# A decoder layer's opening: the third weight's low part moved ahead of the second chunk's average, the fourth weight's first accumulator moved to another PSUM bank, and the first adaLN stage moved to the head of the queue

## The chip, the cores and the metric

One Trainium2 chip, one of its cores. The metric is the device time of one execution in microseconds; a kernel is timed several times and its median is given. The trace comes from one further execution under the hardware profiler.

## The reference

One layer of a decoder trunk for 1024 prompt rows and 8 x 8 sample rows of width 1024, in float32. The opening that the change touches computes, of the reference:

```python
mod = jax.nn.silu(c) @ ada_w[l] + ada_b[l]
shift1, scale1, gate1, shift2, scale2, gate2 = jnp.split(mod, 6, axis=-1)
h = rms_norm(x, norm1_g[l]) * (1.0 + scale1[:, None]) + shift1[:, None]
z = h @ w_in[l]
...
c_y, conf_new = causal_dwconv(c_a * jax.nn.sigmoid(c_b), conf_buf, conf_dw[l])
```

Behind it come retention, sliding-window attention, the convolutions, the output projection and the feed-forward part; the change leaves them as they are.

## The kernel before

**Layout.** The 1088 rows of x stand as columns in `M`, one slice of 128 features each for k = 0 to 7, in three chunks of 384, 384 and 320 columns (`CH`, line 24). A float32 product is made of three products of a reduced format: each operand is split into a high part (a cast on ScalarE) and a low part (a subtraction on VectorE), and TensorE adds high x high, high x low and low x high. `weight_split` (line 245) does this for a block of `w_in`: the cast runs at once, the subtraction at once or, where a list `later` is given, when it is popped from the list. A block of `w_in` is one transfer of 128 x 1024 floats, 512 KB.

**The norm.** `norm1_squares` (438) squares x on ScalarE and adds pairs on VectorE; `norm1` (457) sums them over the features with four products by a matrix of ones, and `rstd` (291) makes the reciprocal root: two functions on ScalarE, three operations on VectorE. `make_h` (471) then makes, for some k, the normed, scaled and shifted x: one multiplication on VectorE (`tmp`), one activation on ScalarE (`hi`), one operation on VectorE (`lo`).

**adaLN in stages.** The first two of the six parts of `mod` are made in four stages of two k each (378). A stage's 2 MB come as four transfers of 512 KB (`stage_load`, 382); stages 0 and 2 use the same room, and so do 1 and 3. `stage_sum` (406) is 32 small products, `stage_copy` (413) a copy on ScalarE, `stage_finish` (420) four products that add pairs, and two operations on VectorE that write shift and scale.

**The order.** From line 987 to 1094 `pinned` is set: ScalarE and VectorE run what stands there in the order of the program, as TensorE does everywhere. Behind line 1094 the order of those two engines is left to the builder, but for the steps of the long convolution (lines 602 to 614), which keep theirs. Transfers are issued by SP, in a queue of its own: x of the first chunk, the first weight, stage 0, the second weight, stage 1, x of the second chunk (397 to 402), the third weight, then what lines 1025 to 1037 ask for. `keep_warm(n)` (990) issues n float32 products that nobody reads, each of which runs as two passes.

**Accumulators.** PSUM has eight banks of 512 columns. `mm_psum` (230) goes round four of them, `misc_psum` (235) round two of the other four until line 1084; the last two are held for the second chunk. The first three weights' accumulators for the first chunk (996) are open from the start. The fourth weight's (1087) is next in the round and so takes the bank of the first weight's, which `evac_c` empties with a sigmoid (588). That sigmoid stands behind the third chunk's norm and a load of its function table (1077 to 1080).

**Around the change** (lines 1020 to 1094): squares and norm of chunk 0, stage 0, h of k 0 and 1, products of the first two weights with it; stage 1, h of k 2 and 3 while the second chunk is squared; norm of the second chunk; h of the second chunk, and so on in turn. The first weight is prepared at line 1022, the second at 1029, with its low part popped between the two weights' products; the third's low part is popped behind the second chunk's norm:

```python
        prepare(2, rest)
        norm1(1, (1, 2, 3))
        rest.pop()()
        make_h(1, (0, 1))
        part(0, (2,), range(4))
```

Of the kernel before, what the change touches and what calls it, by code (L numbers as in the profile page):

```python
# [23 lines left out]
CH = [(0, 384), (384, 384), (768, 320)]  # L24
# [116 lines left out]
def decoder_step(ctx: ExitStack, tc: tile.TileContext, A, O, where):  # L141
# [41 lines left out]
    def nm(s):  # L183
        serial[0] += 1
        return f"{s}_{serial[0]}"
# [10 lines left out]
    def table(name):  # L196
        load = ACT.preload_act_table_set(name)
        for n in group["users"] + ([group["load"].ins.name] if group["load"] else []):
            tc.add_manual_dep(load.ins, n, after, reason="table")
        group["load"], group["users"] = load, []  # L200
# [25 lines left out]
    def bank(kind, n=4):  # L226
        turn[kind] += 1
        return pp.tile([P, 512], F32, tag=f"{kind}{turn[kind] % n}", name=nm(kind))

    def mm_psum(w):  # L230
        return bank("mm")[:, :w]
# [3 lines left out]
    def misc_psum():  # L235
        return bank("pm", misc_banks[0])


    def weight(src, lo_engine, raw=None):
        if raw is None:  # L240
            raw = wp.tile([P, 1024], F32, tag="w", name=nm("w"), bufs=2)
        nc.sync.dma_start(raw, src)
        return raw, lo_engine

    def weight_split(raw, lo_engine, both=None, later=None):
        if both is None:
            hi = wp.tile([P, 1024], F32R, tag="wh", name=nm("wh"), bufs=2)
            lo = wp.tile([P, 1024], F32R, tag="wl", name=nm("wl"), bufs=2)
        else:
            hi, lo = both  # L250
        ACT.copy(hi, raw)
        rest = lambda: lo_engine.tensor_tensor(out=lo, in0=raw, in1=hi, op=ALU.subtract)
        if later is None:
            rest()
        else:
            later.append(rest)
        return hi, lo
# [19 lines left out]
    def act_of(tiles, c):  # L277
        return lambda k: (tiles[c][k // 4][0][:, k % 4, :], tiles[c][k // 4][1][:, k % 4, :])
# [12 lines left out]
    def rstd(ps, w, r, t, e=0):  # L291

        ev = EPS if e == 0 else EPS / 4
        act(r, ps, AF.Ln, bias=eps[:, e : e + 1])
        act(r, r, AF.Exp, scale=-0.5)
        DVE.scalar_tensor_tensor(t, ps, ev, r, ALU.add, ALU.mult)
        DVE.scalar_tensor_tensor(t, t, -0.5, r, ALU.mult, ALU.mult)
        DVE.scalar_tensor_tensor(r, t, 1.5, r, ALU.add, ALU.mult)
# [30 lines left out]
    with ExitStack() as gctx:  # L329
# [5 lines left out]
        def tmp(w=384, dtype=F32):  # L335
            return gp.tile([P, 384], dtype, tag="tmp", name=nm("tmp"), bufs=8)[:, :w]
# [15 lines left out]
        def fetch(i):  # L352
            if i < len(IN_BLOCKS) and i not in loaded:
                raw = None
                if i in (2, 3):
                    tag, n = (("u1", 2 + SEQ + NB * 10), ("t5", NT))[i - 2]
                    raw = gp.tile([P, n], F32, tag=tag, name=nm("w"))[:, 0:1024]
                loaded[i] = weight(A["w_in"][i], DVE, raw)

        def wide(dtype=F32):  # L360
            return gp.tile([P, 1028], dtype, tag="sw", name=nm("sw"), bufs=3)

        def flip(dtype=F32):
            return gp.tile([P, 1024], dtype, tag="pT", name=nm("pT"))

        def prepare(i, later=None):
            if i < len(IN_BLOCKS) and i not in ready:
                fetch(i)
                both = None
                if i == 4:  # L370
                    both = [gp.tile([P, n], F32R, tag=f"t{t}", name=nm("ak"))[:, 0:1024] for t, n in ((4, NT), (5, 1024))]
                elif i in (2, 3, 20, 21):
                    both = (wide(F32R)[:, 0:1024], wide(F32R)[:, 0:1024] if i in (2, 20) else flip(F32R))
                ready[i] = weight_split(*loaded[i], both, later)
                fetch(i + 1)
# [6 lines left out]
        def stage_load(s):  # L382
            k0, k1 = STAGES[s]
            for x, tag in enumerate(ROOM[s]):
                if tag[0] == "t":
                    t = gp.tile([P, NT if tag < "t3" else 1024], F32, tag=tag, name=nm("ada0"))[:, 0:1024]
                else:
                    t = hp.tile([P, 1024], F32, tag=tag, name=nm("ada0"))
                if s < 2:
                    src = A["ada_0"][:, 0:8192].rearrange("p (a k) -> p a k", k=512)[:, 4 * x : 4 * x + 4, k0 * P : k1 * P]  # L390
                    nc.sync.dma_start(t.rearrange("p (a k) -> p a k", a=4), src)  # L391
                else:
                    nc.sync.dma_start(t, A["ada_0"][:, 1024 * (4 * s + x) : 1024 * (4 * s + x + 1)])
                for y in range(4):
                    stage_tiles[s, 4 * x + y] = t[:, 256 * y : 256 * y + 256]

        fetch(0)
        stage_load(0)
        fetch(1)
        stage_load(1)  # L400
        for k in (0, 4):
# [36 lines left out]
        def norm1_squares(c, ks=range(8)):  # L438

            c0, w = CH[c]  # L440
            qs = squares.setdefault(c, [])
            if c < 2 and c not in square_rooms:
                room = [gp.tile([P, 30 + SEQ + NB * 38], F32, tag=f"glu{j}", name=nm("sq")) for j in range(2)]
                square_rooms[c] = [room[j][:, x * w : (x + 1) * w] for j in range(2) for x in range(3)]
            for k in ks:
                q = square_rooms[c][k] if c < 2 and k < 6 else tmp(w)
                ACT.activation(q, M[:, k, c0 : c0 + w], AF.Square)
                if k % 2:
                    DVE.tensor_tensor(out=qs[-1], in0=qs[-1], in1=q, op=ALU.add)
                    if c == 2 and k > 1:  # L450
                        DVE.tensor_tensor(out=qs[0], in0=qs[0], in1=qs.pop(), op=ALU.add)
                else:
                    qs.append(q)
# [3 lines left out]
        def norm1(c, xs=range(4), between=lambda x: None):  # L457
            c0, w = CH[c]
            if c not in sums1:
                sums1[c] = misc_psum()[:, :w]  # L460
            ps, n = sums1[c], len(squares[c]) if c == 2 else 4
            for x in xs[:n]:
                PE.matmul(ps, ones, squares[c][x], start=x == 0, stop=x == n - 1)
                between(x)
            if xs[-1] < 3:
                return
            rstd(ps, w, r1_all[:, c0 : c0 + w], tmp(w))
# [522 lines left out]
        def keep_warm(n, warm=warm):  # L990

            for _ in range(n):
                PE.matmul(warm, ones, ones, start=True, stop=True)

        misc_banks[0] = 2
        acc = {(0, n): mm_psum(CH[0][1]) for n in range(3)}
        free = ["pm2", "pm3"]
        rest = []
        hh, hl, lh = (0, 0), (0, 1), (1, 0)
        count = {}  # L1000

        def terms(c, n, ks, ts):

            ps = acc[c, n]
            for k in ks:
                for i, j in ts:
                    x = count[c, n] = count.get((c, n), 0) + 1
                    PE.matmul(ps, ready[n][i][:, k * P : k * P + P], act_of(h, c)(k)[j], start=x == 1, stop=x == 24)

        def part(c, ns, ks):  # L1010
            for k in ks:
                for n in ns:
                    terms(c, n, (k,), (hh, hl, lh))

        def stage(s):
            ps = misc_psum()
            stage_sum(s, ps)
            return stage_copy(s, ps)

        keep_warm(24)  # L1020
        norm1_squares(0)
        prepare(0)
        norm1(0, between=lambda x: keep_warm(4) if x == 1 else None)
        flat = stage(0)
        stage_load(2)
        keep_warm(5)
        stage_finish(0, flat)
        make_h(0, (0, 1))
        prepare(1, rest)
        keep_warm(8)  # L1030
        part(0, (0,), (0, 1))
        rest.pop()()
        part(0, (1,), (0, 1))
        flat = stage(1)
        stage_load(3)
        fetch(3)
# [9 lines left out]
        keep_warm(5)  # L1046
        part(0, (0, 1), (2, 3))
        prepare(2, rest)
        norm1(1, (1, 2, 3))
        rest.pop()()  # L1050
        make_h(1, (0, 1))
        part(0, (2,), range(4))
        acc[1, 0] = mm_psum(CH[1][1])
# [21 lines left out]
        names = IN_BLOCKS[:4]  # L1075
        part(1, range(3), (6, 7))
        norm1(2)
        table("sigmoid_and_others")
        for n in range(3):
            evac_c(names[n], 0, *CH[0], acc[0, n])  # L1080
# [3 lines left out]
        misc_banks[0] = 4  # L1084
        make_h(2, range(4))
        for c in range(2):
            acc[c, 3] = mm_psum(CH[c][1])
            part(c, (3,), range(8))
            evac_c(names[3], c, *CH[c], acc[c, 3])
            make_h(2, (4 + 2 * c, 5 + 2 * c))  # L1090
# [116 lines left out]
    with ExitStack() as fctx:  # L1207
# [12 lines left out]
        def wide_room(tag):  # L1220
            return up.tile([P, NT], F32, tag=tag, name=nm(tag), bufs=1)
# [187 lines left out]
        acc = wide_room("acc")  # L1409
# [57 lines left out]
        for g in range(NG - 1):  # L1467
# [84 lines left out]
            last = g + 1 == NG - 1  # L1552
# [146 lines left out]
```

## Time and profile before

| | |
|---|---|
| median of 3 runs | 1231.94 us (1231.42 to 1233.59) |
| the profiled execution | 1229.62 us |
| its span, first to last instruction | 1227.6 us |
| mean granted clock of TensorE | 0.997 |
| busy: TensorE, VectorE, ScalarE | 1206.9, 809.7, 464.9 us |
| bytes moved | 113.72 MB, 93 GB/s over the span |

Busy times are sums over the whole span; the opening, the first 90 us or so, has other limits than the rest. The granted clock is 1.00 at 2.4 GHz and 0.50 at 1.2 GHz. All times below are microseconds from the first instruction. Matrix products overlap in the pipeline, so their starts tell more than their lengths.

### The profile page before, as it was taken

The page shows a single profiled execution, that of the slowest core. Times are in us where ns is not written, and L with a number is a line of the kernel's source. Part 1 is how long each engine was busy: PE and PEld are TensorE (multiplying, and loading weights), DVE is VectorE, ACT ScalarE, POOL GpSimd, SP SyncE. Part 2 cuts the span into 40 slices and gives each one's busy share as a digit, 9 for nine tenths or more (in the row PEclk, how much of TensorE's full clock was granted, in tenths as well). Part 3 has the DMA queues.
Part 4 walks back from the last instruction along what each step waited for, and adds up shares of the span by engine and source line. Part 5 has one row for each costly group of instructions (what it writes and reads, how often), then busy time and mean ns, then how long its engine had stood idle before and what let it go on. Part 6 is the DMA issues. An engine that isn't in the chain of part 4 may idle for free.

```text
span 1227.6 us, 17259 instructions
## 1 busy us (share of the span) xinstructions
PE 1206.9 (98%) x7058; PEld 1096.8 (89%) x7058; DVE 809.7 (66%) x1288; ACT 464.9 (38%) x941; POOL 8.5 (1%) x28
## 2 busy tenths in 40 slices
PE   8899999999999999999999999999999999999998
PEld 6787789988899999998999999999999999999887
DVE  4669798884797447736476566566666566566575
ACT  4452333342367324633433333333233333333330
POOL 0000000000000000000000000000000000000000
PEclk9999999999999999999999999999999999999999
DMA  9728811121120723111221211212211221121332
GB/s 344 263 93 316 228 52 52 39 52 35 36 71 18 261 74 116 58 35 52 69 69 52 73 66 62 76 52 70 69 68 53 69 86 52 53 86 52 120 125 90
DMA packets 60165, 113.72 MB, mean 93 GB/s; under 512 B 13495, under 2 KB 29623, under 8 KB 60087
## 3 DMA queue, kind: packets, MB, share of 16 engines
q1 hardware_dynamic: 59943, 112.56, 28.0%
q8 instruction: 55, 0.90, 0.3%
q14 instruction: 23, 0.19, 0.1%
q10 hardware_dynamic: 144, 0.07, 0.0%
HBM read 101.90 MB, written 10.72 MB: 92 GB/s over the span
## 4 chain that ended last, share of the span: by engine, by line
PE 88%; DVE 7%; ACT 2%; SPq 1%; DMA 1%; issue 1%; DVEq 0%
PE ps L171 48%; PE mm L171 30%; PE pm L171 6%; DVE x L158 3%; PE sm L171 3%; PE pm L175 1%; PE ada L171 1%; DMA M<-in_xT 1%; SPq L391 1%; DVE al L158 1%; DVE ql L158 1%; ACT ah L158 1%; ACT q L158 0%; DVE qh L305 0%; DVE lo L312 0%
## 5 line engine op out<-in xcount | busy, mean ns | idle before, releaser
L171 PE MATMUL ps<-hi,wl 128*128 128x384 f32 (+1 forms) x672 | 219.5, 327 | 0.0
L171 PE MATMUL ps<-hi,wh 128*128 128x384 f32 (+1 forms) x672 | 219.3, 326 | 0.0
L171 PE MATMUL ps<-lo,wh 128*128 128x384 f32 (+1 forms) x672 | 219.1, 326 | 0.0
L171 PE MATMUL mm<-hi,wh 128*128 128x384 f32 (+1 forms) x544 | 181.4, 333 | 0.0
L171 PE MATMUL mm<-hi,wl 128*128 128x384 f32 (+1 forms) x544 | 177.6, 326 | 0.6 <-DVE wl L158 0.6
L171 PE MATMUL mm<-lo,wh 128*128 128x384 f32 (+1 forms) x544 | 177.5, 326 | 0.2 <-DVE lo L158 0.2
L158 ACT ACTIVATE q<-ps 128x384 f32<-128x384 f32 (+1 forms) x112 | 42.5, 380 | 351.7 <-PE ps L171 351.7
L158 DVE TENSOR_TENSOR x<-x,ps 128x512 f32<-128x512 f32 x264 | 165.1, 679 | 0.4 <-PE ps L171 0.4
L171 PE MATMUL ps<-qh,al 128*128 128x512 f32 x408 | 159.6, 391 | 0.0
L171 PE MATMUL ps<-ql,ah 128*128 128x512 f32 x408 | 159.5, 391 | 0.0
L171 PE MATMUL ps<-qh,ah 128*128 128x512 f32 x408 | 158.9, 389 | 0.0
L171 PEld LDWEIGHTS ps<-hi,wh 128*128 128x128 f32 x672 | 126.2, 188 | 2.2
L171 PEld LDWEIGHTS ps<-lo,wh 128*128 128x128 f32 x672 | 126.1, 188 | 2.2
L171 PEld LDWEIGHTS ps<-hi,wl 128*128 128x128 f32 x672 | 126.1, 188 | 0.0
L171 PEld LDWEIGHTS mm<-hi,wh 128*128 128x128 f32 x544 | 102.1, 188 | 8.0 <-issue 6.8
L171 PEld LDWEIGHTS mm<-hi,wl 128*128 128x128 f32 x544 | 102.1, 188 | 0.9 <-DVE wl L158 0.9
L171 PEld LDWEIGHTS mm<-lo,wh 128*128 128x128 f32 x544 | 102.2, 188 | 0.5 <-DVE lo L158 0.5
L158 DVE TENSOR_TENSOR wl<-fr,wh 128x1024 fp32r<-128x1024 f32 x27 | 33.1, 1224 | 101.8 <-ACT wh L158 101.8
L614 DVE SCALAR_TENSOR_TENSOR M<-glu,cmix,M 128x512 f32<-128x512 f32 (+2 forms) x150 | 97.7, 666 | 2.0
L171 PEld LDWEIGHTS ps<-qh,al 128*128 128x128 f32 x408 | 76.6, 188 | 16.1
L171 PEld LDWEIGHTS ps<-ql,ah 128*128 128x128 f32 x408 | 76.6, 188 | 14.8
L171 PEld LDWEIGHTS ps<-qh,ah 128*128 128x128 f32 x408 | 76.6, 188 | 14.6
(344 smaller groups left out, 1824.4 us busy)
## 6 DMA issues: line engine op xcount, KB each, us to landing
w<-in_w_ff SPq DMA_DIRECT2D x29, 512.0 KB, 3.7
ar<-in_w_ff SPq DMA_DIRECT2D x28, 512.0 KB, 3.7
fr<-in_w_ff SPq DMA_DIRECT2D x28, 512.0 KB, 3.6
w<-in_w_in SPq DMA_DIRECT2D x22, 512.0 KB, 5.1
M<-in_ada SPq DMA_DIRECT2D x20, 512.0 KB, 4.9
ada<-in_ada SPq DMA_DIRECT2D x16, 512.0 KB, 10.5
sw<-in_ada SPq DMA_DIRECT2D x9, 512.0 KB, 4.3
w<-in_w_out SPq DMA_DIRECT2D x8, 512.0 KB, 3.6
```

Of the source, the lines that this page charges most:

```text
L158: i = f(*args, **kw)
L171: return tc.keep_in_program_order(nc.tensor.matmul(*args, **kw))
L175: return tc.keep_in_program_order(nc.tensor.transpose(*args, **kw))
L391: nc.sync.dma_start(t.rearrange("p (a k) -> p a k", a=4), src)
L614: DVE.scalar_tensor_tensor(dst, src(t), cdw[:, j, t : t + 1], dst, ALU.mult, ALU.add))))
```

## The change

Five edits, all in the opening:
- stage 0 of adaLN is loaded ahead of the first weight;
- the first weight is prepared behind stage 0's sum, with its low part put off, and three fillers stand there in place of five;
- the first two weights' products with k 0 and 1 are regrouped: the low parts of both weights are made behind h, and the terms that use them stand behind the four groups that don't;
- the third weight's low part stands ahead of the last three sums of the second chunk's norm;
- the fourth weight's first accumulator is taken from `misc_psum` behind the third chunk's norm.

```diff
@@ -394,8 +394,8 @@
+        stage_load(0)
         fetch(0)
-        stage_load(0)
         fetch(1)
         stage_load(1)
         for k in (0, 4):
@@ -1019,18 +1019,21 @@
         keep_warm(24)
         norm1_squares(0)
-        prepare(0)
         norm1(0, between=lambda x: keep_warm(4) if x == 1 else None)
         flat = stage(0)
         stage_load(2)
-        keep_warm(5)
+        prepare(0, rest)
+        keep_warm(3)
         stage_finish(0, flat)
         make_h(0, (0, 1))
         prepare(1, rest)
         keep_warm(8)
-        part(0, (0,), (0, 1))
-        rest.pop()()
-        part(0, (1,), (0, 1))
+        rest.pop(0)()
+        rest.pop(0)()
+        terms(0, 0, (0, 1), (hh, hl))
+        terms(0, 1, (0, 1), (hh, hl))
+        terms(0, 0, (0, 1), (lh,))
+        terms(0, 1, (0, 1), (lh,))
         flat = stage(1)
@@ -1046,8 +1049,8 @@
         prepare(2, rest)
+        rest.pop()()
         norm1(1, (1, 2, 3))
-        rest.pop()()
         make_h(1, (0, 1))
         part(0, (2,), range(4))
@@ -1075,6 +1078,7 @@
         part(1, range(3), (6, 7))
         norm1(2)
+        last = misc_psum()[:, : CH[0][1]]
         table("sigmoid_and_others")
@@ -1084,7 +1088,7 @@
         for c in range(2):
-            acc[c, 3] = mm_psum(CH[c][1])
+            acc[c, 3] = mm_psum(CH[c][1]) if c else last
             part(c, (3,), range(8))
             evac_c(names[3], c, *CH[c], acc[c, 3])
```

## Rows read from the trace of the kernel before

**Rows 1.** Waits of TensorE, 0 to 150 us: total, times, longest.

```profile
PE mm L171 <- DVE sw L158: 3.8, 1, 3.8
PE mm L171 <- ACT M L158: 2.9, 1, 2.9
```

**Rows 2.** Chain of waits, first 150 us: start, length, what.

```profile
14.34 11.27 DMA M<-in_xT
...
57.04 3.65 PE mm L171 x21
...
66.22 0.50 ACT M L158
...
66.77 18.46 PE mm L171 x96
```

**Rows 3.** Timeline, 15 to 28 us: start, length, engine, what, [idle before, releaser].

```profile
15.19 0.64 PE L171 MATMUL pm<-ada,sc 128*32 128x256 f32 x8 [0.86 <-DMA ada<-in_ada]
15.76 1.38 PE L171 MATMUL mm<-ones 128*128 128x128 f32 x10
...
22.07 0.45 PE L171 MATMUL mm<-hi,wl 128*128 128x384 f32 x1 [0.58 <-DVE wl L158]
...
25.64 0.94 ACT L158 ACTIVATE sq<-M 128x384 f32<-128x384 f32 x2 [0.30 <-DMA M<-in_xT]
...
27.31 0.88 PE L171 MATMUL pm<-sq,ones 128*128 128x384 f32 x2 [0.76 <-DVE sq L158]
```

**Rows 4.** Windows, 10 to 20 us; the last column is GB/s.

```profile
10.00:20.00 10.00, 8.56 (x77) 5.80 (x75) 5.12 (x11) 3.17 (x7) 0.00 (x0) 1.00 1.09 357
```

**Rows 5.** Timeline, 31 to 42 us, ScalarE, VectorE and TensorE.

```profile
31.27 1.03 ACT L158 CAST sw<-w 128x1024 fp32r<-128x1024 f32 x1
...
34.54 0.56 DVE L158 SCALAR_TENSOR_TENSOR tmp<-pm,r 128x384 f32<-128x384 f32 x1 [2.59 <-ACT r L158]
...
36.20 1.22 DVE L158 TENSOR_TENSOR sw<-w,sw 128x1024 fp32r<-128x1024 f32 x1
37.33 1.14 DVE L158 SCALAR_TENSOR_TENSOR tmp<-M,a,r 128x384 f32<-128x384 f32 x2
...
37.47 0.62 PE L171 MATMUL mm<-hi,sw 128*128 128x384 f32 x2 [3.79 <-DVE sw L158]
...
38.63 1.15 DVE L158 SCALAR_TENSOR_TENSOR lo<-tmp,mod,hi 128x384 fp32r<-128x384 f32 x2 [0.16 <-ACT hi L158]
...
41.56 0.34 PE L171 MATMUL mm<-lo,wh 128*128 128x384 f32 x1
```

**Rows 6.** Timeline: stage 3's shift on VectorE, the third chunk's average on TensorE.

```profile
52.32 0.20 DVE L158 TENSOR_TENSOR mod<-pm,cfirst 128x36 f32<-128x36 f32 x1
...
63.15 0.70 PE L171 MATMUL pm<-tmp,ones 128*128 128x320 f32 x2
```

**Rows 7.** Windows: length, busy PE, PEld, DVE, ACT, POOL; granted clock, DMA share, GB/s.

```profile
33.70:37.47 3.77, 0.00 (x0) 0.00 (x1) 2.86 (x5) 0.77 (x2) 0.00 (x0) 1.00 1.02 404
66.38:69.79 3.41, 3.02 (x9) 3.02 (x10) 2.39 (x5) 3.39 (x6) 0.00 (x0) 0.50 0.00 0
```

**Rows 8.** Timeline, 76 to 87 us, VectorE and TensorE.

```profile
76.85 0.56 DVE L158 TENSOR_TENSOR glu<-mm,M 128x384 f32<-128x384 f32 x1 [1.07 <-PE mm L171]
...
82.18 0.56 DVE L284 TENSOR_TENSOR tmp<-tmp,tmp 128x384 fp32r<-128x384 f32 x1 [0.79 <-ACT tmp L283]
...
85.06 0.51 PE L171 MATMUL pm<-tmp,exact 128*128 128x384 f32 x2
...
86.79 0.56 DVE L296 SCALAR_TENSOR_TENSOR tmp<-pm,tmp 128x384 f32<-128x384 f32 x1 [3.38 <-ACT tmp L203]
```

**Rows 9.** Window 90 to 131 us, and steps of the convolution on VectorE there.

```profile
90.00:131.00 41.00, 41.00 (x270) 32.23 (x266) 39.26 (x62) 12.23 (x22) 0.94 (x2) 1.00 0.87 281
...
119.88 6.04 DVE L614 SCALAR_TENSOR_TENSOR M<-glu,cmix,M 128x512 f32<-128x512 f32 x9
```

**Rows 10.** Timeline of GpSimd from the start.

```profile
1.13 0.29 POOL L1097 CAST exact<-ones 128x128 fp32r<-128x128 f32 x1
```

## Prediction

> **What bounds the kernel now.** I read the waits of TensorE first, because it is busy nearly everywhere and an idle stretch of it is the time that can be had. In the first 150 us two waits stand out: 3.8 us for VectorE's `sw` (the low part of the third weight) and 2.9 us for ScalarE's `M` (a sigmoid) [rows 1]. The chain of waits over the same stretch says which of the many small waits ahead of them count: from 14.34 us it is the transfer of the second chunk of x, for 11.27 us, and only then the engines [rows 2]. The timeline shows how close the engines are behind it: ScalarE waits 0.30 us for that transfer and starts squaring at 25.64 [rows 3]. So ahead of 25.64 the transfer is the bound, behind it the chain of engines. Last I read the clock by stretch, because the two idle stretches were not alike: the one from 33.70 kept the full clock (1.00), the one from 63.85 was followed by 3.41 us at 0.50, that is 1.2 GHz in place of 2.4, with nine products in it [rows 7].
>
> **Part 1: the opening up to 25.64 us (first adaLN stage first, first weight later, pairs of terms regrouped, filler 5 to 3).** SP issues the same transfers as before; the four of adaLN stage 0 pass one of 512 KB. At 357 GB/s, the rate of this stretch [rows 4], its 0.524 MB are 1.47 us, so the stage's last quarter, for which TensorE waits 0.86 us until 15.19 [rows 3], lands some 1.5 us earlier, by estimate, and the first weight where that quarter landed. Two fillers less are four of the passes of which ten take 1.38 us, 0.55. So h of k 0 and 1 comes 2.0 us earlier. The terms with both low parts now stand behind all terms with high parts, so that TensorE waits for a `wl` (0.58 us idle ahead of 22.07 [rows 3]) with less left to do; but the first weight's low part, done before stage 0 until now, joins this piece, so I count about half a microsecond back: the second stage's sum starts some 1.5 us earlier.
> The change adds waits too. ScalarE now waits, between the copy of stage 0 and h, for the first weight to land (about 15.2, cast of 1.03 us); behind it stand both h of k 0 and 1, the cast of the second weight and the copy of stage 1. On VectorE both low parts (1.23 us each) stand behind these h and ahead of stage 1's shift; on TensorE the last two terms wait for them and the second stage's sum stands behind. I cost all of this at **nothing**, gain and loss: the cover is the second chunk of x. Ahead of it on the queue lies the same set of bytes, in another order, so I leave its landing at 25.64; behind it come two squares on ScalarE, their addition on VectorE, for which TensorE waits 0.76 us until the sum at 27.31 [rows 3], and nothing of the change stands between. If the landing moves, it moves everything after it one for one. The trace does not show the transfers in the new order; its nearest rows are one transfer of 512 KB, 1.4 to 1.5 us, either way: earlier by as much as the engines have gained, later by as much if the small pieces of stage 0 slip past. I take 0, because sum and rate are those of before; both ends go into the range.
>
> **Part 2: the third weight's low part ahead of the average.** VectorE is idle 2.59 us before it can begin the reciprocal root at 34.54 [rows 5]. The cast that the low part needs ends at 31.27 + 1.03 = 32.30, and the subtraction takes 1.22 us, so it now runs from 32.32 to 33.55, a microsecond before 34.54: the root is not held up. If that cover were gone (third weight late), the average would be late one for one. TensorE's products that stood until 37.47 (idle 3.79) go on at 33.60: -3.87 us. What is late next is h of the second chunk. VectorE is rid of the 1.22 us at 36.20, so `tmp` moves from 37.33 to 36.20 (-1.13) and `lo` from 38.63 to 37.50; two take 1.15, the first is there at 38.08. TensorE, done with stage 2's sum, wants the product with that `lo` at 41.56 - 3.87 = 37.69 and gets it at about 38.15 [rows 5]. So -3.41 is left. The next pieces have room: from the first `tmp` to the last `lo` of a pair pass 2.45 us (37.33 to 39.78), so k 2 and 3, begun at 38.6, are there by 41.0; TensorE wants k 2 eighteen products and a stage's four small ones after 38.15, near 41.5. Behind stage 3 ScalarE and VectorE wait for TensorE and move with it. **Term: -3.4 us.**
>
> **Part 3: the bank.** In the kernel before the fourth weight's first accumulator takes the bank of the first weight's, which the sigmoid empties at 66.72 [rows 2]. TensorE ends the third chunk's average at 63.85 and idles 2.92 us until 66.77. The new bank is one of two; its last reader is VectorE's shift of stage 3 at 52.32, long past [rows 6]. The 24 products start at once: **-2.9 us**. The next accumulator now takes the bank that the sigmoid empties, by then 63.3, and is wanted at 64.65: no wait.
> With the idle stretch goes the low clock behind it. The run of 96 products from 66.77 takes 18.46 us, and 21 products at the full clock take 3.65, 0.174 each [rows 2]; 96 of these are 16.7, and the run's last product shows 0.17 of tail, so the nine at half clock cost 18.46 - 16.7 - 0.2 = **-1.5 us**. TensorE would then be 3.4 + 2.9 + 1.5 = 7.8 us ahead.
>
> **Part 4: what the third chunk gives back.** VectorE moves by the 3.4 us of part 2 only, plus its own idle: 1.07 us at 76.85 for the product that now comes sooner, and 0.79 at 82.18 [rows 8]: 5.3 in all. Its subtraction for the first key norm is done at 82.74 - 5.3 = 77.5; TensorE's average of it stood at 85.06, and would like to run at 77.3. So 0.25 to 0.3 is given back. Behind it VectorE has 3.38 us idle at 86.79 [rows 8], and catches up. **Term: +0.3 us.**
> From there on no transfer sets a time: the loads of the second adaLN follow the products that free their room. I leave the rest of the kernel as it was.
> **Sum:** 0 - 3.4 - 2.9 - 1.5 + 0.3 = -7.5 us. The profiled execution took 1229.62 us, of which the span is 1227.6; it becomes 1222.1. The median of the runs is 2.3 us over it, so I forecast 1231.94 - 7.5 = **1224.4**.
>
> **A rule that speaks against it.** The idle stretch of 0.76 us ahead of 27.31 grows to about 2.3: TensorE is done with its filler some 1.5 us earlier and still waits for the squares. Of two idle stretches of before, the longer one (3.77 us without a product) kept the clock, the shorter (2.92) lost it [rows 7]. The Trainium skill, TensorE: Matmul & The Clock Gate, section on HAM oscillation, says that waits between bursts throw the engine back to the low clock, so that the next burst begins slow; by the page's rule alone the sum here would be -6.0, one such burst more, and the trace agrees with it in one of the two cases.
>
> **The rivals.**
> A: **the clock falls at 27 us.** For it: about 2.3 us without work, little less than the stretch that lost it; against: the one of 3.77 that did not. Price as in part 3, 1.5 us on the way to the average's sum: 1225.9.
> B: **VectorE gives more back.** From 90 to 131 us it is busy 39.26 of 41 us, TensorE all the time [rows 9]; if it doesn't catch up at 86.79, what is left is its own movement by 77 us, 3.4 + 1.07 = 4.5: 1227.4. For it that share; against it the 3.38 idle.
> C: **the bank is not free**, the change does not do what it says: a rotation that I miscounted leaves the sigmoid in front. Only part 2 is left: 1228.5.
> D: **the gain is lost again**, all of it, where VectorE is that full: about 1231.9. For and against it what stands at B.
> E: **slower.** Behind the opening the program's order isn't pinned: a copy written at line 1097 runs at 1.13 us [rows 10]. If the order of VectorE's work comes out otherwise, a norm that TensorE waits for may stand behind convolution steps. Nine in a row take 6.04 us, 0.67 each [rows 9]; 11 of them eat the 7.5, and two blocks of nine give 12.1 - 7.5 = +4.6: 1236.5. For it that VectorE has no room there; against it that the steps of the convolution keep their order and the change touches none.
>
> **How the numbers follow.** Forecast 0.60, A 0.13, B 0.13, C 0.04, D 0.04, E 0.06. The forecast's own range is 1222.4 to 1225.9: 1.5 us either way for the landing, and half a microsecond for the runs' spread below. The range reaches over A and B to C: 1222.4 to 1228.6; D, E and a part of B lie outside. A measurement of this kernel tells apart about 0.2%, 2.5 us, so faster ends at 1229.5. Faster: forecast, A, most of B (0.10) and of C (0.03), 0.86; the rest of B and C with D, same, 0.08; slower E, 0.06.
>
> **What would show it.** Right: no wait for `sw` near 33 to 37; TensorE without a gap at the third average and no half clock after it; squares of the second chunk at 25.6 as before; `lo` of the second chunk at 37.5; the first key norm's average near 77.5. The opening's first products should stand about 2 us earlier and buy nothing. Wrong: squares at another time than 25.6 (part 1), a new wait of TensorE between 77 and 150 us (B, D, E), half clock from 27 us (A), the sigmoid still in front of the fourth weight (C).

## The result and the profile after

| | before | changed |
|---|---|---|
| median, same chip | 1232.03 us (4 runs) | 1222.95 us (4 runs, 1222.25 to 1224.72) |
| the profiled execution | 1229.62 us | 1222.88 us |
| its span | 1227.6 us | 1220.8 us |
| mean granted clock of TensorE | 0.997 | 0.999 |

The ratio is 0.9927, interval 0.9909 to 0.9944: faster by 9.1 us. The profiled executions differ by 6.7 only. The difference of 2.4 us between the two is a question of its own, which the experiments answer.

The waits of TensorE, changed kernel, first 150 us (engine, line waited for: total, times, longest):

```profile
PE pm L171 <- DVE sq L158: 1.5, 1, 1.5
...
PE pm L171 <- DVE tmp L284: 0.9, 1, 0.9
PE pm L171 <- DMA ada<-in_ada: 0.6, 1, 0.6
```

The two large waits [rows 1] are gone. The longest one left, 1.5 us for `sq`, is the wait for the second chunk of x, which had been 0.76 us [rows 3]. The 0.9 us for L284 is no new wait: the kernel before has the same line, with the same numbers, in this stretch.

The chain of waits in the changed kernel, opening (start, length, what):

```profile
14.70 10.98 DMA M<-in_xT
25.71 0.94 ACT sq L158 x2
...
59.18 5.79 PE pm L171 x32
64.98 8.43 PE mm L171 x48
73.49 0.49 ACT tmp L659
```

The transfer still ends at 25.7, as before (25.6 [rows 2]): the opening's engines run earlier, the first product with h of k 0 at 17.53 in place of 19.34, and buy nothing. From 59.18 to 73.49 the chain is TensorE without a break; the sigmoid `M` is no longer on it.

The timeline of the changed kernel where the gain arises (start, length, engine, what, [idle before, releaser]):

```profile
27.38 0.89 PE L171 MATMUL pm<-sq,ones 128*128 128x384 f32 x2 [1.47 <-DVE sq L158]
...
32.39 1.22 DVE L158 TENSOR_TENSOR sw<-w,sw 128x1024 fp32r<-128x1024 f32 x1 [0.38 <-ACT sw L158]
...
34.61 0.56 DVE L158 SCALAR_TENSOR_TENSOR tmp<-pm,r 128x384 f32<-128x384 f32 x1 [1.00 <-ACT r L158]
...
37.70 1.15 DVE L158 SCALAR_TENSOR_TENSOR lo<-tmp,mod,hi 128x384 fp32r<-128x384 f32 x2 [0.15 <-ACT hi L158]
...
38.37 0.44 PE L171 MATMUL mm<-lo,wh 128*128 128x384 f32 x1 [0.21 <-DVE lo L158]
...
60.07 0.70 PE L171 MATMUL pm<-tmp,ones 128*128 128x320 f32 x2
60.36 0.58 PE L171 MATMUL pm<-hi,sw 128*128 128x384 f32 x1
```

The low part (32.39) fits into VectorE's idle time and the root starts at 34.61, as before (34.54 [rows 5]). The product with the second chunk's `lo` stands at 38.37, not 41.56 [rows 5], and the third chunk's average at 60.07, not 63.15 [rows 6]: 3.08 us. The fourth weight's first product follows the average at once.

Windows of the changed kernel (length, busy PE, PEld, DVE, ACT, POOL; granted clock, DMA share, GB/s):

```profile
33.70:37.47 3.77, 3.77 (x43) 2.61 (x42) 2.75 (x5) 1.27 (x3) 0.07 (x1) 1.00 1.03 411
66.38:69.79 3.41, 3.41 (x21) 3.41 (x21) 3.16 (x8) 2.50 (x5) 0.00 (x0) 1.00 0.76 240
90.00:131.00 41.00, 41.00 (x269) 32.35 (x269) 33.44 (x53) 9.85 (x19) 0.94 (x2) 1.00 0.91 271
```

Both idle stretches [rows 7] are full of products, and none of it runs at 0.50. The third row is for comparison with the kernel before [rows 9]; everything here stands some 7 us earlier, so it does not hold the same work.

Last, the end of the opening, where part of the gain was given back; first TensorE, then VectorE and ScalarE of the changed kernel:

```profile
77.44 0.51 PE L171 MATMUL pm<-tmp,exact 128*128 128x384 f32 x2
78.18 0.41 PE L171 MATMUL mm<-hi,wh 128*128 128x320 f32 x1 [0.23 <-ACT hi L158]
78.64 0.42 PE L171 MATMUL mm<-lo,wh 128*128 128x320 f32 x1
...
73.49 0.49 ACT L659 ACTIVATE tmp<-mm 128x384 f32<-128x384 f32 x1 [1.29 <-PE mm L171]
73.88 0.90 ACT L158 ACTIVATE hi<-tmp,mod 128x256 fp32r<-128x256 f32 x2
...
74.41 0.88 DVE L158 SCALAR_TENSOR_TENSOR lo<-tmp,mod,hi 128x256 fp32r<-128x256 f32 x2 [0.44 <-ACT hi L158]
...
75.81 0.55 DVE L284 TENSOR_TENSOR tmp<-tmp,tmp 128x384 fp32r<-128x384 f32 x1
...
78.16 0.76 DVE L158 TENSOR_TENSOR lo<-M,hi 128x256 fp32r<-128x256 f32 x2 [0.47 <-ACT hi L158]
```

The rows of the kernel before that answer to them, beside the average at 85.06 [rows 8]:

```profile
85.41 0.31 PE L171 MATMUL mm<-hi,wh 128*128 128x320 f32 x1
85.56 0.30 PE L171 MATMUL mm<-lo,wh 128*128 128x320 f32 x1
...
82.66 0.75 DVE L158 TENSOR_TENSOR lo<-M,hi 128x256 fp32r<-128x256 f32 x2
```

The average moved by 7.62 us (85.06 to 77.44), the next product but one by 6.92 (85.56 to 78.64). VectorE's `lo` of the sample rows moved by 4.5 only (82.66 to 78.16), and TensorE now waits 0.23 us for ScalarE's `hi` of those rows and then for this `lo`.

### The profile page after: what moved, and what is told of

Read it like the earlier page. It is cut to its first block, busy times and chain, and to the rows that moved or that the text cites. A ratio compares the mean times of both kernels' runs of the same rounds, so it can differ in the third digit from the quotient of the medians.

```text
span 1220.8 us, 17251 instructions
## 1 busy us (share of the span) xinstructions
PE 1206.5 (99%) x7054; PEld 1095.5 (90%) x7054; DVE 809.7 (66%) x1288; ACT 465.0 (38%) x941; POOL 8.2 (1%) x28
## 4 chain that ended last, share of the span: by engine, by line
PE 87%; DVE 8%; ACT 2%; SPq 1%; DMA 1%; issue 1%; DVEq 0%; ACTq 0%
PE ps L171 47%; PE mm L171 29%; PE pm L171 6%; DVE x L158 3%; PE sm L171 3%; PE pm L175 1%; PE ada L171 1%; DMA M<-in_xT 1%; SPq L391 1%; DVE al L158 1%; ACT ah L158 1%; DVE ql L158 1%; ACT q L158 0%; DVE qh L305 0%; DVE lo L312 0%
```

## The experiments

My theory after the result: the gain is the two idle stretches and the low clock behind them, each for itself, and the opening adds nothing. The rivals: the opening has a part in it; the parts depend on each other; or the low clock is not what separates the timed 9.1 us from the profiled 6.7.

### The parts of the change, alone

**The bank alone.**

```diff
+        last = misc_psum()[:, : CH[0][1]]
         table("sigmoid_and_others")
...
-            acc[c, 3] = mm_psum(CH[c][1])
+            acc[c, 3] = mm_psum(CH[c][1]) if c else last
```

> The kernel before with the bank alone. Main theory (each part is worth what the trace shows): the idle 2.92 us and the 1.5 us of low clock behind it go, some 0.5 is given back where VectorE has to keep up in the third chunk, so 3.9 us faster in the profile (span about 1223.7). Rival (the third chunk is bound by VectorE): VectorE's own idle there is 1.07 + 0.79, so not over 2 us faster.

Measured: 1226.61 us against 1231.36 for the kernel before, ratio 0.9963 (0.9949 to 0.9976), -4.75. The average is followed at once, but the wait for the third weight's low part stays, and in this execution its idle stretch does lose the clock, as it had not in the profile of before. Its windows, columns as above:

```profile
33.70:37.70 4.00, 0.24 (x2) 0.00 (x0) 2.83 (x5) 1.03 (x2) 0.00 (x0) 1.00 1.03 407
37.70:41.11 3.41, 3.38 (x10) 3.06 (x10) 3.24 (x6) 1.15 (x2) 0.10 (x1) 0.50 1.04 376
```

The loss shows in the third chunk's average, which had stood at 63.15 [rows 6] behind the same program:

```profile
64.94 0.70 PE L171 MATMUL pm<-tmp,ones 128*128 128x320 f32 x2
```

The rival's bound of 2 us is passed. The spans differ by 3.0 us (1227.6 to 1224.6) and not by the theory's 3.9; this execution has the loss at 37.70, which the profile of before had not.

**The low part alone.**

```diff
         prepare(2, rest)
+        rest.pop()()
         norm1(1, (1, 2, 3))
-        rest.pop()()
```

> The kernel before with the third weight's low part ahead of the average and nothing else. Main theory: 3.1 us faster (the third average 3.1 us earlier, all behind it moved as one), span about 1224.5; the idle 2.92 us ahead of the fourth weight stays. Rival 1 (the opening has to be early for it): under 2 us. Rival 2 (in timed runs the clock falls in the idle stretch at 33.7 us too, which the profiled execution did not show): the timed difference is 1 to 2 us larger than that of the profiled spans.

Measured: 1226.69 us, ratio 0.9958 (0.9945 to 0.9970), -4.67. The wait for the sigmoid is left, 2.9 us. The spans differ by 3.0 us (1227.6 to 1224.6), about the theory's 3.1, and the timed difference is 1.7 larger, the size that rival 2 asks for. The agreement of the span is in part chance: this execution kept the clock behind the sigmoid's wait, where that of before lost it, and fell to 0.50 at one place more, at 550 us, during a wait of 2.25 us.

**The opening alone** (the first three edits).

```diff
+        stage_load(0)
         fetch(0)
-        stage_load(0)
...
+        prepare(0, rest)
+        keep_warm(3)
...
+        terms(0, 0, (0, 1), (hh, hl))
+        terms(0, 1, (0, 1), (hh, hl))
+        terms(0, 0, (0, 1), (lh,))
+        terms(0, 1, (0, 1), (lh,))
```

> The change without its bank and without the low part's move: stage 0 first, first weight later, terms regrouped. Main theory: 0 within 0.5 us; ScalarE squares the second chunk at 25.6 to 25.7 as before, having waited about 1 us for it. Rival (the 2.3 us by which the timed difference of 9.1 is larger than that of the two profiled spans, 6.8, come from the opening): 2.3 us faster.

Measured: 1231.79 us over 11 runs, ratio 1.0001 (0.9992 to 1.0010). The chain of waits and the timeline of this kernel:

```profile
14.55 11.04 DMA M<-in_xT
...
25.62 0.94 ACT L158 ACTIVATE sq<-M 128x384 f32<-128x384 f32 x2 [1.01 <-DMA M<-in_xT]
```

The transfer lands as before and ScalarE has waited 1.01 us for it, as the main theory said; the rival's 2.3 us did not come.

**The other two without the opening.** It is the sum of the first two diffs.

> The change without the opening's part: bank and low part alone. Main theory: as the whole change, 1223 us within 0.5 (squares of the second chunk at 25.6, third average near 60). Rival (the opening counts): 2 us slower than the whole change.

Measured: 1222.09 us, ratio 0.9923 (0.9911 to 0.9936), -9.27. This is the whole gain. The two parts alone add to 9.42, so neither needs the other, and the opening is worth nothing within what can be told. The profiled span, 1220.8 us, is that of the changed kernel.

### What the low clock costs

Fillers put into an idle stretch leave the wait as it is and keep TensorE at work. **One stretch filled**, the one behind the third chunk's average:

```diff
         norm1(2)
+        keep_warm(10, misc_psum()[:, :P])
         table("sigmoid_and_others")
```

> The kernel before with ten products that nobody reads (2.8 us of work) in TensorE's idle stretch ahead of the fourth weight; the wait for the sigmoid stays. Theory (the low clock behind this stretch has a price of its own): up to 1.5 us faster than before, in those executions in which the clock fell there; no half clock between 64 and 72 us in the trace. Rival (the clock there costs nothing, the products wait for VectorE anyway): same time as before within 0.3 us.

Measured: 1230.28 us (11 runs), ratio 0.9982 (0.9973 to 0.9991), -2.1, more than the theory's 1.5. The 11 executions fall into three groups: four at 1228.8 (clock 0.998), two at 1230.3 (0.997), five at 1231.1 to 1231.6 (0.995). The profiled one, of the first group, kept the clock at the filled stretch and lost it behind the one that was not filled:

```profile
37.98:41.39 3.41, 3.41 (x18) 2.68 (x20) 2.78 (x6) 1.15 (x2) 0.00 (x0) 0.50 1.05 371
41.39:45.00 3.61, 3.61 (x42) 2.73 (x35) 1.05 (x2) 1.39 (x3) 0.00 (x0) 1.00 1.06 395
```

So the slower executions, at lower mean clocks, lost more than this one stretch; where is not recorded.

**Both filled**, the other diff being

```diff
         make_h(1, (0, 1))
+        keep_warm(13)
         part(0, (2,), range(4))
```

> As the fill of the third stretch, and thirteen such products (3.6 us) in the idle stretch ahead of the third weight's low part at 33.7 us; both waits stay. Theory (in timed runs the clock falls behind both stretches; this is the difference between 9.1 us timed and 6.8 us in the spans): 2.5 to 3.5 us faster than before, mean clock 0.998 or more. Rival (the clock falls at the second stretch seldom): as the fill of the third alone.

Measured: 1228.60 us, ratio 0.9971 (0.9959 to 0.9982), -3.8, a little over the theory's range. The two work in the places meant (timeline, TensorE):

```profile
33.27 3.06 PE L171 MATMUL mm<-ones 128*128 128x128 f32 x26
37.57 0.62 PE L171 MATMUL mm<-hi,sw 128*128 128x384 f32 x2 [0.89 <-DVE sw L158]
...
63.79 2.39 PE L171 MATMUL pm<-ones 128*128 128x128 f32 x20
66.87 0.45 PE L171 MATMUL mm<-hi,sw 128*128 128x384 f32 x1 [0.69 <-ACT M L158]
```

The products behind them start where they had (37.47 [rows 5], 66.77 [rows 2]), so the 3.8 us are the low clock alone (2.2 to 5.1 by the interval): 2.1 with the stretch behind the third average filled, by difference 1.7 for the third weight's wait. The intervals of the two runs overlap, so this split is rough, but the traces agree with it: the third chunk's average stands at 63.25 here, without a loss, at 64.75 with one stretch filled and at 64.94 with the bank alone, each with 3.41 us at 0.50, and at 65.50 with the opening alone, with 6.8. One loss there costs 1.5 to 1.8 us, the longer one 2.3. With this the timed 9.1 us close, as far as the medians go: 3.08 + 2.92 of idle time, less 0.7 to 0.8 given back, is some 5.3; and 3.8 of low clock.

### What bounds the opening

**The second chunk queued behind the third weight**, one transfer of 512 KB, in the changed kernel:

```diff
+        fetch(2)
         for k in (0, 4):
             nc.sync.dma_start(M[:, k : k + 4, 384:768], xT[:, k : k + 4, 384:768])
-        fetch(2)
```

> The changed kernel with the third weight's transfer ahead of the second chunk of x on the queue. Theory (the landing of the second chunk is the bound of the opening, one for one): squares of the second chunk at 27.1 us in place of 25.7, 1.4 us slower than the changed kernel, about 1224.3. Rival (the engines bind the opening, with a microsecond of room): the same as the changed kernel within 0.4 us.

Measured: 1225.78 us, ratio 0.9945 (0.9932 to 0.9959), 2.8 over the changed kernel's median, 2.2 by the ratios; the two intervals overlap. The theory said 1.4. In the profiled execution the squares are 1.25 us later (25.71 to 26.96), the third chunk's average 4.1 (60.07 to 64.17), and the rest is clock:

```profile
26.96 0.94 ACT L158 ACTIVATE sq<-M 128x384 f32<-128x384 f32 x2 [2.29 <-DMA M<-in_xT]
...
25.00:27.80 2.80, 0.88 (x8) 0.69 (x7) 0.37 (x2) 0.84 (x2) 0.00 (x0) 1.00 1.07 385
27.80:31.20 3.40, 2.57 (x8) 1.99 (x9) 2.91 (x6) 2.25 (x6) 0.00 (x0) 0.50 1.03 409
31.20:34.60 3.40, 3.40 (x14) 3.40 (x14) 2.49 (x4) 2.41 (x5) 0.00 (x0) 0.50 1.03 411
```

So the transfer bounds this stretch, and the longer wait of TensorE behind it, 2.75 us for the squares, does what rival A said.

**The second chunk and the third weight ahead of adaLN stage 1**, with the chunk's norm and the third weight's products with k 0 and 1 moved ahead of that stage's sum, and the pieces that stood there put behind it:

```diff
-        stage_load(1)
         for k in (0, 4):
...
         fetch(2)
+        stage_load(1)
...
+        norm1_squares(1)
+        prepare(2, rest)
+        rest.pop()()
+        norm1(1, between=lambda x: keep_warm(4) if x < 3 else None)
+        make_h(1, (0, 1))
+        part(0, (2,), (0, 1))
         flat = stage(1)
```

> The changed kernel with the second chunk of x and the third weight ahead of adaLN stage 1 on the queue, and the second chunk's norm ahead of stage 1 in the program, so that h of the second chunk for k 0 and 1 is made before stage 1 is there. Theory (the opening is bound by the order of the transfers): second chunk squared from about 20.5 us, the third chunk's average some 3.5 us earlier, 1219 to 1220. Rival (the bytes up to stage 1 bind, whatever their order): within 0.7 us of the changed kernel.

Measured: 1222.53 us, ratio 0.9924 (0.9912 to 0.9936): a miss, no better than the changed kernel. The chunk is squared six microseconds sooner, but TensorE takes fillers between the four sums, idles behind stage 1's sum, and loses the clock:

```profile
19.56 1.35 ACT L158 ACTIVATE sq<-M 128x384 f32<-128x384 f32 x3 [0.52 <-DMA M<-in_xT]
...
31.44 0.45 PE L171 MATMUL mm<-hi,wh 128*128 128x384 f32 x1 [1.40 <-ACT hi L158]
...
32.30:35.70 3.40, 3.40 (x13) 3.40 (x13) 0.31 (x2) 0.00 (x0) 0.00 (x0) 0.50 1.03 411
```

The low clock is not the whole of the miss: the profiled execution is the slowest of the five (1223.73 us), and those with mean clocks of 0.999 and 1.000 took 1222.1 to 1222.5, about the changed kernel's fastest, 1222.25, also at 1.000.

**The same with fewer fillers.** Of the twelve between the four sums three are left, and three more stand behind stage 1's sum.

```diff
-        norm1(1, between=lambda x: keep_warm(4) if x < 3 else None)
+        norm1(1, between=lambda x: keep_warm((0, 2, 1, 0)[x]))
         make_h(1, (0, 1))
-        part(0, (2,), (0, 1))
+        terms(0, 2, (0, 1), (hh, hl))
+        terms(0, 2, (0, 1), (lh,))
         flat = stage(1)
+        keep_warm(3)
```

> The second chunk's rows and the third weight still land ahead of the first adaLN stage, and the fillers between the first weight's and the second's sums are cut from ten to three. Theory (in the run before, the early rows were worth nothing because the fillers stood ahead of the chunk's average on TensorE): the average stands about 2.3 us earlier than there, the idle 1.40 us at 31.44 goes, the third chunk's average comes about 2 to 3 us earlier than in the changed kernel, span about 1217.5 to 1218.5, timed about 1219 to 1220. Rival (the bytes of the opening, or the first adaLN stage that now comes last, bound it): TensorE waits as long for the stage's rows as it wins, and the time stays within 0.7 us of the changed kernel, 1222.3 to 1223.6.

Measured: 1221.17 us against 1232.04, ratio 0.9915 (0.9901 to 0.9928). The idle 1.40 and the low clock are gone, but the third chunk's average stands at 59.41 against 60.07, 0.66 us earlier and not 2 to 3. The rival holds in the trace: stage 1's rows now come last.

```profile
27.85 0.64 PE L171 MATMUL pm<-ada,sc 128*32 128x256 f32 x8 [0.20 <-DMA ada<-in_ada]
29.34 0.64 PE L171 MATMUL pm<-ada,sc 128*32 128x256 f32 x8 [0.85 <-DMA ada<-in_ada]
29.91 0.94 PE L171 MATMUL mm<-ones 128*128 128x128 f32 x6
...
59.41 0.70 PE L171 MATMUL pm<-tmp,ones 128*128 128x320 f32 x2
```

The time itself lies between the two ranges, 1.8 us under the changed kernel's median. The average explains 0.66 of it; besides, this profiled execution kept the clock at a place near 316 us where that of the changed kernel lost it (last section). In these runs the order of the transfers decides which of them TensorE waits for; it changes little in how long. This version has the lowest median of all, but its interval and the changed kernel's overlap, so that it beats that one is not shown.

### What was given back

**The sample rows' work ahead of the last conditioning chunks**, so that VectorE's `lo` of them is not its last work:

```diff
         make_h(2, range(4))
+        x = M[:, :, SEQ:]
...
+        modulated_sample(h, x, a1, mod[:, 0:8, :])
         for c in range(2):
...
-        x = M[:, :, SEQ:]
...
-        modulated_sample(h, x, a1, mod[:, 0:8, :])
```

> The changed kernel with the sample rows' multiplication and modulation ahead of the two conditioning chunks, so that they no longer stand with VectorE's last work before the block's first residual addition. Theory (0.7 to 0.8 us of the gain was given back because VectorE's low part for the second run of the block came last): the give-back shrinks, the block's slot starts 0.5 to 0.7 us earlier, timed about 1222.3. Rival (VectorE's total up to there is the same, and the builder only puts other work into the place): within 0.2 us of the changed kernel.

Measured: 1223.12 us, ratio 0.9926 (0.9914 to 0.9939): the rival, no change in the median. In the profiled execution the product that stood at 78.64 comes at 79.33, and the span is 0.7 us longer (1221.5). The `lo` is now made by 73.6, and the key norm's own operands (those of the average that stood at 77.44), behind the work put off, are what TensorE waits for:

```profile
77.66 0.49 ACT L283 CAST tmp<-tmp 128x384 fp32r<-128x384 f32 x1
...
78.30 0.41 PE L171 MATMUL pm<-tmp,exact 128*128 128x384 f32 x1 [0.75 <-ACT tmp L283]
78.91 0.44 PE L171 MATMUL pm<-tmp,exact 128*128 128x384 f32 x1 [0.20 <-DVE tmp L284]
```

**Both of the last two edits together.**

> Both edits at once. If each acts at a place of its own, the two gains add: by the theories some 3 to 4 us under the changed kernel, 1218.5 to 1219.5. If VectorE's queue up to the block's first residual addition is what binds in both, the sum is no better than the larger of the two.

Measured: 1222.22 us, ratio 0.9921 (0.9907 to 0.9934). The gains don't add; there was none of the second to add. That the amount of VectorE's work between the third average and the key norm binds there, and not its order, is what these two orders suggest. It is not shown: no run took work away, and the longest wait in the other order is for a cast on ScalarE (77.66).

## Why the prediction was right, and where it was not

The direction, the two causes and the place of each were right; the time came 1.45 us below the forecast of 1224.4, inside the range (1222.4 to 1228.6).

- **Part 1, nothing:** right. The opening alone gives 1.0001, the other parts without it the whole gain. The wait for `sq` grew from 0.76 to 1.47 us while the landing stayed at 25.7, as the text expected in kind. It said 2.3: the first product with h came 1.81 us earlier and stage 1's sum 1.45 (22.97 to 21.52), near the 2.0 and 1.5 of the text, but that sum then waits 0.59 us for its own transfer, which the text had not counted.
- **Part 2, -3.4:** -3.08 at the third average (63.15 to 60.07). The product with the late `lo` came at 38.37, the text said 38.15.
- **Part 3, the bank, -2.9:** right; the average and the product behind it touch. **The low clock, -1.5:** in the profiled execution 7.62 - 3.08 - 2.92 = 1.6, close.
- **Part 4, +0.3:** mis-sized, 0.7 by the first products behind (7.62 against 6.92), 0.8 by the spans (7.62 against 6.8). The step that failed took the key norm's L284 for VectorE's last work. That one moved by 6.4 us (82.18 [rows 8] to 75.81); the builder put it between the sample rows' multiplications, and ScalarE's L659 ahead of an `hi`, for which VectorE idles 0.44 us at 74.41. The sample rows' `lo` came last. The experiment with the other order has the same median. The sign "the first key norm's average near 77.5" came, at 77.44, but not for the text's reason: its operand was there at 76.36, and the average ran when TensorE came to it, with no give-back; that stands one product behind it.
- **The sum:** its arithmetic on the profiled execution was good, 1222.1 against 1222.88. The step that failed is the next one, "The median of the runs is 2.3 us over it, so I forecast 1231.94 - 7.5". It took those 2.3 us for a fixed distance. They were low clock, as far as the runs show: the timed executions of the kernel before have mean clocks of 0.994 to 0.997, most of them under the 0.997 of the profiled one. The stretch at 33.70, which kept the full clock in the profiled execution of before [rows 7], lost it in that of three other kernels with the same stretch (the bank alone, the opening alone, one stretch filled). Where each timed execution lost it is not recorded. The change removes that stretch too, and with it some 1.7 us that the sum did not hold: the clock term of part 3 should have been 3.8 for two stretches, by the run with both filled, and not 1.5 for one. That the forecast came as near as 1.45 us is in part luck: the sum for the profiled execution had 0.8 us too much gain, in parts 2 and 4, and the step to the median 2.2 us too little.
- **Rival A** did not come in the changed kernel: 1.47 us of idle ahead of 27.38 kept the clock. Its mechanism is real; with the chunk 1.25 us later the clock fell at 27.8. The rule of the Trainium skill, TensorE: Matmul & The Clock Gate, section on HAM oscillation, that waits between bursts throw the next burst back to the low clock, agrees with the runs where 1.2 GHz followed a wait: 2.8 us with the chunk later, 2.9 in the kernel before, 3.8 with the bank alone. The stretch of 3.77 us that kept the clock [rows 7] shows that it isn't so each time, and the last section has a place where the clock fell with no wait ahead of it.
- **Rivals B and D** did not come, but not because VectorE had more room: over the same work, 83 to 124 us in the changed kernel, it is busy 39.20 of 41 us, as before (39.26 [rows 9]). TensorE is busy 41.00 in both and has no wait between 90 and 130 us. VectorE's idle time ahead of L296, 3.38 us before [rows 8], shrank to 0.58 (at 79.50): it caught up there, as part 4 said. **C** and **E** did not come either: the bank was free, and the time fell.

## What to carry to other kernels

An idle stretch of TensorE that loses the clock in some executions is worth more than its own length, and one profile may show it at its cheapest: before a sum is moved from the profiled execution to the median, ask what the difference between these two consists of. Filling the stretch with products that nobody reads measures that part by itself, since it leaves the wait as it is. And where a transfer bounds, as here, another order of the engines' work ahead of it bought nothing, and another order of the transfers mostly changed which one is waited for.

## What the runs showed of the hardware that was not expected

The same idle stretch of 3.8 us, at the same place in the program, kept the clock in one profiled execution and lost it, for 3.4 us or more at 1.2 GHz, in three. The stretch of 2.92 us lost it in two (the kernel before, the opening alone) and kept it with the low part alone. A wait of 1.40 us was followed by 1.2 GHz with the chunk first, one of 1.47 us in the changed kernel was not. With the opening alone the clock fell inside the stretch of 3.8 us, at 35.80, and stayed until 42.62 (windows):

```profile
35.80:37.46 1.66, 0.00 (x0) 0.00 (x0) 1.66 (x3) 0.00 (x0) 0.00 (x0) 0.51 1.04 415
37.46:42.62 5.16, 5.16 (x26) 3.86 (x30) 3.21 (x6) 1.15 (x2) 0.10 (x1) 0.50 1.05 376
42.62:45.00 2.38, 2.38 (x28) 1.73 (x21) 0.30 (x1) 1.22 (x3) 0.00 (x0) 0.99 1.05 402
```

The clock also fell where TensorE had not waited. Two windows of the changed kernel, columns as above:

```profile
313.00:315.00 2.00, 2.00 (x66) 1.98 (x63) 0.70 (x3) 0.27 (x1) 0.00 (x0) 1.00 0.03 8
315.00:318.50 3.50, 3.50 (x31) 2.71 (x31) 3.36 (x8) 1.82 (x5) 0.00 (x0) 0.65 0.00 0
```

From 316.06 to 319.47 the clock was 0.50; TensorE has no wait between 290 and 320 us, and ahead of the fall it ran some 60 products of eight columns each. At the same place of the program the clock fell in five of the thirteen profiled executions (the kernel before at 322.37, the changed kernel, the low part alone, the two parts without the opening, the sample rows early). The change does not touch this place, and as both profiles of the main comparison have the loss, it does not enter their difference; it can enter the medians. Of the two parts without the opening the profiled execution, with the loss, took 1222.92 us, the other four, at mean clocks of 1.000, 1221.89 to 1222.17.

The executions of one kernel differ in steps: 1228.8, 1230.3 and 1231.1 to 1231.6 us with one stretch filled. What decides between them no run here shows. Over the whole span the kernel before had mean clocks of 0.994 to 0.997, the changed kernel, without the two idle stretches, 0.997 to 1.000.
